# Hybrid decoder layer in split fp32: another order of the seven-product pairs, and eight of them per group instead of seven

## The chip, the cores and the metric

The kernel runs on one core of a Trainium2 chip. The metric is the device time of one execution in microseconds (us). The engines are named as in the profile: PE multiplies matrices, DVE and ACT are the vector and the scalar engine, POOL is GpSimd, SP issues most of the DMA transfers.

## What is computed

One layer over 272 tokens (16 learned ones and 256 given ones) with a model width of 4096, and a last norm:

```
h = rmsnorm(x, norm_g)
q, k, v, g_attn, b_conv, c_conv, h_conv, z_conv = split(h @ w_in)      # 8 x 2048 columns
o = stick_breaking_attention(heads(q), heads(k), heads(v))             # 16 heads x 128
o = group_rmsnorm(o * silu(g_attn), attn_norm_g, ATTN_HEADS)
y = b_conv * short_conv(c_conv * h_conv, conv_w)                       # 16 groups x 128
y = group_rmsnorm(y * silu(z_conv), conv_norm_g, CONV_GROUPS)
x = x + concatenate([o, y]) @ w_out                                    # 4096 x 4096
return rmsnorm(x, final_norm_g)[:, N_META:]
```

All of it is fp32. `w_in` is 4096 x 16384 and `w_out` 4096 x 4096.

## The kernel before

**Split products.** PE multiplies operands of a shorter type (fp32r), so each fp32 operand is split in a high part (a cast, on ACT, L308) and a low part (operand minus high part, on DVE, L309). One product is three matmuls: token low part by weight high part (L340), high by high (L342), high by low (L343).

**Pieces.** The weights come as pieces of 128 x 1024 (512 KB) in one list, `pieces`. For each piece the program loads it (SP, `load`, 8 pieces ahead), splits it (`split`, 5 pieces ahead; `wh` and `wl` have six buffers each, the raw pieces five) and multiplies with it (`mm_in`). A piece is named by a letter, its group and its pair; in the profile it is a number, as in `wl92`. The scheduler of the framework fixes each engine's order of instructions from this program before the run.

**Groups.** Two attention heads and two conv channel groups make one of 8 groups. A group has two stages. In the first, the 32 blocks of 128 model rows are taken as 16 pairs j, each with pieces A and B; the outputs are four PSUM banks (two halves of the tokens by two halves of the columns), `D11`, `D12`, `D21`, `D22`. In the second, eight plain blocks (k, v, c, h of two heads or channel groups) take four pieces of 24 matmuls each (`mm`, L332 to L334).

**Seven products.** A pair of blocks is a 2 x 2 product of blocks: eight products, 24 matmuls of 128 x 512, or seven products, 21 matmuls, with sums of tokens and sums of weights in place of the eighth. The pairs of `SJ` (groups 1 to 7) and of `OUT_SJ` (the output blocks) are done so. They need the token sums `sum{j}` (POOL L228 to L231, then split by ACT L232 and DVE L233), and of the weights, per group: t (L317, 128 x 1024), two more sums of 128 x 512 (L320 and L321), and the splits of T (which is t) and U (the last sum) as pieces of their own. Of B only one half is split. The order of such a pair is A, B, T, U; its products go partly into four more banks, `P1`, `P5`, `P6`, `P7`.

**End of a first stage.** After U of the last seven-product pair, `evict_sums` adds these four banks up (ACT L516, DVE L517 to L520); two more pieces later `evict` (L526) adds them to the four others. The four transposes of `mix` (`mxc`, L570) and the first plain block need banks that L518 and L520 set free.

**Group 0** has no seven-product pairs. There the tokens themselves are prepared: for each j, `prep_x` multiplies a piece of x by the norm's weight (L211, L213) and splits it (L218, L219); if j is in `SJ`, the token sums follow at once. After the pairs 4 to 12 a piece of x in rows is squared for the norm (L281). The sums are kept for all groups.

**Tasks.** All else (gates, scores, weights of the attention, conv, norms, the transposes of the results) is tied to piece numbers by `later`. The results of groups 0 to 6 go to memory (`mixd`) and are loaded again as pieces m; those of group 7 stay. Its `conv_out` (L544, L547) is on POOL, its norm on ACT (L557, L564) and DVE (L559, L173 to L182, L561), and its transposes `mxc7` (L570) stand at piece n1 + 8.

**Output stage.** Three blocks of 1024 output columns, as groups 8, 9 and 10, take 16 pairs each, in the order `OUT_ORDER`; the tokens' place is taken by the results, `mixh` and `mixl`. In group 8 the pieces m4, m5 and m6 come in between; each of them is split (L286, L287), and token sums `osum{j}` are made of it. Loads of the residual and the last norm's weight are issued at two pairs of each block (`load_res`). Then come the last 1024 columns with plain products (`mo`).

Of the kernel before, what the change touches and what calls it, by code (L numbers as in the profile page):

```python
# [17 lines left out]
KC = D // P  # L18
# [7 lines left out]
GROUPS = 8  # L26
# [11 lines left out]
WARM = 10  # L38
LOADS, SPLITS, RING = 8, 5, 6

SJ = (2, 4, 6, 8, 10, 12, 14)


OUT_ORDER = (0, 1, 2, 3, 8, 4, 9, 5, 10, 6, 11, 7, 12, 13, 14, 15)
OUT_SJ = (8, 9, 10, 11, 12, 13)


def seven(g, j):
    return j in (OUT_SJ if g >= GROUPS else SJ if g else ())

# [6 lines left out]
def kernel(ctx, tc, xt, xin, xm, par, fg, w1, w2, out):  # L57
# [35 lines left out]
    pieces = []  # L93
    ends = {}
    fin = {}
    ms = [("m", g) for g in range(GROUPS - 1)]
    for g in range(GROUPS):
        for j in range(KC // 2):
            pieces += [(q, g, j) for q in ("ABTU" if seven(g, j) else "AB")]
            if g == 0 and 4 <= j < 13:  # L100
                pieces.append(("x", j - 4))
        fin[g] = len(pieces) - 1
        for u, b in ((0, 0), (0, 1), (1, 0), (1, 1), (0, 2), (0, 3), (1, 2), (1, 3)):
            for kc in range(4):
                pieces.append(("p", (2 * g + u, b), kc))
            ends.setdefault(g, []).append(len(pieces) - 1)
            if g == GROUPS - 1 and b == 2 + u:
                pieces += ms[2 * u:2 * u + 2]
    n1 = len(pieces)

    for g in range(GROUPS, GROUPS + 3):
        for at_, j in enumerate(OUT_ORDER):
            for q in "ABTU" if seven(g, j) else "AB":
                pieces.append((q, g, j))
                if g == GROUPS and (at_, q) in ((2, "A"), (3, "A"), (9, "A")):
                    pieces.append(ms[{2: 4, 3: 5, 9: 6}[at_]])
        fin[g] = len(pieces) - 1
    for nb in range(6, 9):
        for kc in range(16 if nb < 7 else 8):
# [74 lines left out]
    sp = sctx.enter_context(tc.tile_pool(name="sp", bufs=1))  # L194
    S = {j: sp.tile([P, 2, 4, P], F32R, name=f"sum{j}") for j in SJ}
    xr = {}
# [8 lines left out]
    def prep_x(j, parts=1):  # L205
# [11 lines left out]
        if parts == 1:  # L217
            nc.scalar.copy(out=x[:, :, 0, :], in_=t)  # L218
            nc.vector.tensor_tensor(out=x[:, :, 1, :], in0=t, in1=x[:, :, 0, :].bitcast(F32), op=ALU.subtract)  # L219
        if j in SJ:  # L220
            token_sums(S[j], t[:, :, META:], j)

    def token_sums(dst, t, j):
        a11, a21 = t[:, 0, :P], t[:, 0, P:]
        a12, a22 = t[:, 1, :P], t[:, 1, P:]
        f = wk.tile([P, 4, P], F32, tag="u2", name=f"sf{j}", bufs=2)
        v = nc.gpsimd
        v.tensor_tensor(out=f[:, 0, :], in0=a21, in1=a22, op=ALU.subtract)  # L228
        v.tensor_tensor(out=f[:, 2, :], in0=a11, in1=a21, op=ALU.subtract)
        v.tensor_tensor(out=f[:, 1, :], in0=f[:, 0, :], in1=a11, op=ALU.subtract)  # L230
        v.tensor_tensor(out=f[:, 3, :], in0=a12, in1=f[:, 1, :], op=ALU.add)  # L231
        nc.scalar.copy(out=dst[:, 0], in_=f)  # L232
        nc.vector.tensor_tensor(out=dst[:, 1], in0=f, in1=dst[:, 0].bitcast(F32), op=ALU.subtract)  # L233
# [13 lines left out]
    def load(i):  # L247
        p = pieces[i]
        if p[0] in "TU":
            return  # L250
        if p[:2] == ("A", 0) and p[2] > 0:
            load_x(p[2])
        t = wp.tile([P, 1024], F32, tag="raw", name=f"raw{i}", bufs=5)
        raws[i] = t
        if p[0] == "x":
            if p[1] < 8:
                r, c = divmod(p[1], 4)
                nc.sync.dma_start(out=t, in_=xin[r * P:(r + 1) * P, c * 1024:(c + 1) * 1024])
            else:
                nc.sync.dma_start(out=t[:, :512], in_=xm)  # L260
        elif p[0] == "m":
            nc.sync.dma_start(out=t.rearrange("p (a b) -> p a b", a=4), in_=mixd[p[1]])
        elif i < 2:
            for h in range(2):
                nc.sync.dma_start(out=t[:, 512 * h:512 * h + 512], in_=where[i][:, 512 * h:512 * h + 512])
                if i == 0 and h == 0:
                    nc.sync.dma_start(out=xr[0][:, 1:, :], in_=xt[:, 1:2, :])
        else:
            nc.sync.dma_start(out=t, in_=where[i])
# [131 lines left out]
    def run_tasks(i):  # L401
        ready = [t for t in tasks if t[0] <= i]
        for t in ready:
            tasks.remove(t)
        for t in sorted(ready, key=lambda t: t[0]):
            t[1](*t[2])

    V, A, G, T = nc.vector, nc.scalar, nc.gpsimd, nc.tensor
# [85 lines left out]
    def plain_block(u, b, e):  # L494
        ps = psum.pop((u, b, "p"))
        if b == 0:
            k_block(u, ps[:, :L])
        elif b == 1:
            v_block(u, ps[:, :L], e + 4 if u % 2 == 0 else e + 2)
        elif b == 2:  # L500
            c_block(u, ps[:, META - 2:L])
        else:
            h_block(u, ps[:, META - 2:L], e + 1)


    gr = {}
# [201 lines left out]
    def cols(nb):  # L708
        return (nb * 512, 512) if nb < 7 else (3584 + (nb - 7) * 256, 256)

    def load_res(nb):
        c, w = cols(nb)
        for t in range(2):
            nc.sync.dma_start(out=res[t][:, c:c + w], in_=xin[t * P:(t + 1) * P, c:c + w])
        if nb % 2 == 0 or nb == 7:
            fgs["tile"] = wk.tile([P, 1024], F32, tag="cb1", name=f"fg{nb}")
        o = 512 * (nb % 2) if nb < 7 else 256 * (nb - 7)
        f = fgs["tile"][:, o:o + w]
        nc.sync.dma_start(out=f, in_=fg[:, c:c + w].broadcast_to([P, w]))
        fgs[nb] = f  # L720
# [86 lines left out]
    for i in range(1 - SPLITS, n):  # L807

        ahead = min(4, max(0, i - (n - 16) + 5))
        while loaded < min(i + LOADS + ahead + 1, n):  # L810
            load(loaded)
            loaded += 1
        while halved < min(i + SPLITS + ahead + 1, n):
            split(halved)
            halved += 1
        if i < 0:
            continue
        p = pieces[i]
        if i < n1:
            mm_in(i)  # L820
            if p[0] == "p" and p[2] == 3:
                plain_block(*p[1], i)
            if p[0] == ("U" if p[1] else "B") and p[2] == SJ[-1]:
                evict_sums(p[1])
                if p[1] == GROUPS - 1:
                    open_mix(0)
            if i in fin.values():
                evict(pieces[i][1])
            if i == n1 - 1:
                open_tail()  # L830
        elif p[0] in "ABTU":
            mm_in(i)
            g = p[1]
            if p[0] == "B" and p[2] in (10, 6):
                load_res(2 * (g - GROUPS) + (p[2] == 6))
            if p[0] == "U" and p[2] == OUT_SJ[-1]:
                out_sums(g)
            if i == fin[g]:
                for q, nb, t in ((D11, 0, 0), (D12, 1, 0), (D21, 0, 1), (D22, 1, 1)):
                    psum["o", 2 * (g - GROUPS) + nb, t] = psum.pop((g, q))  # L840
                for nb in range(2):
                    for t in range(2):
                        out_block(2 * (g - GROUPS) + nb, t)
        elif p[0] == "o":
            if "all" not in hd:
                hd["all"], turn[0] = True, 4
            _, nb, kc = p
            final = nb == 8
            mm_out(i, (0,) if final else (0, 1))
            if kc == 3:  # L850
                load_res(nb)
            if kc == (15 if nb < 7 else 7):
                for t in (0,) if final else (0, 1):
                    out_block(nb, t)
        run_tasks(i)
# [8 lines left out]
def _w1(w_in, np):  # L864

    w = w_in.reshape(KC, P, 8, HEADS, P).transpose(2, 3, 1, 0, 4)
    q, k, v, g, b, c, h, z = w
    kinds = (k, v, c, h)
    out = []
    for gr in range(GROUPS):  # L870
        us = 2 * gr, 2 * gr + 1
        n1 = [t[u] for u in us for t in (q, g)]
        n2 = [t[u] for u in us for t in (b, z)]
        for j in range(KC // 2):
            k1, k2 = 2 * j, 2 * j + 1
            out.append(np.concatenate([t[:, k1] for t in n1] + [t[:, k2] for t in n2], axis=1))
            out.append(np.concatenate([t[:, k2] for t in n1] + [t[:, k1] for t in n2], axis=1))
        for u, kind in ((0, 0), (0, 1), (1, 0), (1, 1), (0, 2), (0, 3), (1, 2), (1, 3)):
            for kc in range(4):
                out.append(kinds[kind][us[u]][:, 8 * kc:8 * kc + 8].reshape(P, 1024))  # L880
    return np.ascontiguousarray(np.stack(out))
# [49 lines left out]
```

## Time and profile before

| | |
|---|---|
| runs | 1829.32, 1831.61, 1831.73 us; median 1831.61 us |
| profiled execution | 1833.59 us, of which its span is 1831.7 us |
| mean granted clock of PE | 0.996 |
| PE, DVE, ACT, POOL busy | 1809.7, 1355.4, 1072.8, 111.6 us |
| first stage of group 0 | from 7.49 to 97.84 us |
| first stages of groups 1 to 7, from the first matmul of 128 x 512 to the first of the plain blocks | 83.20, 85.27, 83.16, 83.00, 82.96, 82.96, 83.31 us |
| output blocks 8, 9 and 10 | from 1473.44 to 1731.18 us |

The profile was taken in one execution, and its times count from the start of the span. In a timeline a row has the start, the duration, engine, line, operation, and what is written and read; an "x3" joins three of a kind. Neighbouring instructions of an engine overlap by some 0.08 us, and matmuls by more, so that the step from one start to the next is what an instruction costs. In brackets stands the idle time of the engine before the row and what ended it. A view of windows has for each stretch its length, the busy time of each engine with its number of instructions, the granted clock of PE (1.00 is full), the busy share of the DMA engines and GB/s.

### The profile page before, as it was taken

What the parts mean: (1) busy time and instruction counts of PE and PEld (TensorE: products, weight loads), DVE (VectorE), ACT (ScalarE), POOL (GpSimd) and SP (SyncE); (2) the same over time, 40 slices, a digit from 0 to 9 for tenths busy, and PEclk for the clock granted to TensorE, in tenths of its full rate; (3) what the DMA queues carried; (4) which work ended last, traced back from release to release, by engine and by line L of the source; (5) the groups of instructions that cost most, each with busy time, mean ns of one, the idle gap of its engine ahead of it and who ended that gap; (6) DMA issues with size and microseconds to landing.
All of it is one profiled execution on the core that took longest, in us unless ns stands there. A gap on an engine that the chain in (4) does not pass through costs nothing.

```text
span 1831.7 us, 29345 instructions
## 1 busy us (share of the span) xinstructions
PE 1809.7 (99%) x11121; PEld 1633.6 (89%) x11121; DVE 1355.4 (74%) x1969; ACT 1072.8 (59%) x1653; POOL 111.6 (6%) x172
## 2 busy tenths in 40 slices
PE   9999999999999999999999999999999999999997
PEld 7799889988998899889988998899889977888887
DVE  6686786678667876786678667866786768898953
ACT  6766556655665666556655665566556655555542
POOL 2210001000100010001000100010001031000000
PEclk9999999999999999999999999999999999999999
DMA  8865566446554664466546644755475675665663
GB/s 295 303 213 167 164 219 204 169 161 205 201 173 157 218 207 168 167 220 202 170 159 222 206 169 162 227 195 170 165 231 185 208 261 197 232 227 193 225 216 120
DMA packets 106846, 364.26 MB, mean 199 GB/s; under 512 B 11984, under 2 KB 16848, under 8 KB 106704
## 3 DMA queue, kind: packets, MB, share of 16 engines
q1 hardware_dynamic: 102672, 358.72, 58.7%
q10 hardware_dynamic: 4032, 3.67, 0.6%
q8 instruction: 87, 1.43, 0.3%
q14 instruction: 55, 0.45, 0.1%
HBM read 354.48 MB, written 7.86 MB: 198 GB/s over the span
## 4 chain that ended last, share of the span: by engine, by line
PE 93%; DVE 2%; ACT 1%; DMA 1%; issue 1%; POOL 1%; SPq 0%; POOLq 0%; DVEq 0%; ACTq 0%
PE P L343 15%; PE P L340 15%; PE P L342 15%; PE mm L332 14%; PE mm L333 13%; PE mm L334 13%; PE mo L755 2%; PE mo L756 2%; PE mo L754 2%; DVE wl L309 2%; ACT wh L308 1%; DMA xr<-xt 0%; PE z L602 0%; PE po L648 0%; DMA raw<-xin 0%
## 5 line engine op out<-in xcount | busy, mean ns | idle before, releaser
L309 DVE TENSOR_TENSOR wl<-raw,wh 128x1024 fp32r<-128x1024 f32 (+1 forms) x707 | 810.8, 1172 | 270.9 <-ACT wh L308 257.8
L308 ACT CAST wh<-raw 128x1024 fp32r<-128x1024 f32 (+1 forms) x707 | 690.2, 1005 | 543.0 <-PE mm L333 209.7
L332 PE MATMUL mm<-xs,wh 128*128 128x258 f32 (+1 forms) x2048 | 590.7, 288 | 1.6 <-DVE cb L520 1.5
L333 PE MATMUL mm<-xs,wh 128*128 128x258 f32 (+1 forms) x2048 | 583.3, 285 | 0.0
L334 PE MATMUL mm<-xs,wl 128*128 128x258 f32 (+1 forms) x2048 | 583.1, 285 | 0.0
L332 PEld LDWEIGHTS mm<-xs,wh 128*128 128x128 f32 x2048 | 386.7, 189 | 5.0 <-ACT wh L308 1.6
L333 PEld LDWEIGHTS mm<-xs,wh 128*128 128x128 f32 x2048 | 386.8, 189 | 0.6
L334 PEld LDWEIGHTS mm<-xs,wl 128*128 128x128 f32 x2048 | 386.8, 189 | 0.0
L340 PE MATMUL P<-wh,xs 128*128 128x512 f32 x779 | 304.4, 391 | 2.4 <-ACT wh L308 2.4
L343 PE MATMUL P<-wl,xs 128*128 128x512 f32 x779 | 303.6, 390 | 1.1 <-DVE wl L309 1.1
L342 PE MATMUL P<-wh,xs 128*128 128x512 f32 x779 | 303.4, 390 | 0.0
L340 PEld LDWEIGHTS P<-wh,xs 128*128 128x128 f32 x779 | 146.3, 188 | 32.6 <-ACT wh L308 3.3
L343 PEld LDWEIGHTS P<-wl,xs 128*128 128x128 f32 x779 | 146.3, 188 | 32.4 <-DVE wl L309 1.9
L342 PEld LDWEIGHTS P<-wh,xs 128*128 128x128 f32 x779 | 146.4, 188 | 30.0
L343 PE MATMUL P<-wl,mixh 128*128 128x512 f32 x294 | 115.5, 393 | 0.5 <-DVE wl L309 0.5
L340 PE MATMUL P<-wh,mixl 128*128 128x512 f32 x294 | 115.5, 393 | 0.4 <-ACT wh L308 0.4
L342 PE MATMUL P<-wh,mixh 128*128 128x512 f32 x294 | 115.2, 392 | 0.0
L317 DVE TENSOR_TENSOR t<-raw,raw 128x1024 f32<-128x1024 f32 x67 | 81.9, 1223 | 20.8 <-DMA raw<-w 17.8
L308 ACT CAST wh<-t 128x1024 fp32r<-128x1024 f32 x67 | 70.6, 1054 | 43.6 <-PE P L342 30.4
L309 DVE TENSOR_TENSOR wl<-t,wh 128x1024 fp32r<-128x1024 f32 x67 | 82.1, 1225 | 3.4 <-ACT wh L308 2.6
L340 PE MATMUL P<-wh,sum 128*128 128x512 f32 x196 | 76.3, 390 | 0.0
L342 PE MATMUL P<-wh,sum 128*128 128x512 f32 x196 | 76.3, 389 | 0.0
(243 smaller groups left out, 1806.3 us busy)
## 6 DMA issues: line engine op xcount, KB each, us to landing
raw<-w SPq DMA_DIRECT2D x638, 512.0 KB, 4.0
raw<-xin SPq DMA_DIRECT2D x8, 512.0 KB, 5.0
xr<-xt SPq DMA_DIRECT2D x15, 272.0 KB, 5.2
raw<-mixd SPq DMA_DIRECT2D x7, 512.0 KB, 3.9
res<-xin SPq DMA_DIRECT2D x14, 256.0 KB, 6.1
out<-res SPq DMA_DIRECT2D x4, 512.0 KB, 3.3
mixd<-mfh ACTq DMA_DIRECT2D x14, 128.0 KB, 2.4
mixd<-mfc ACTq DMA_DIRECT2D x14, 128.0 KB, 3.8
```

The lines of the kernel that those rows point to most:

```text
L308: nc.scalar.copy(out=h[:, c], in_=t[:, c])
L309: nc.vector.tensor_tensor(out=lo[:, c], in0=t[:, c], in1=h[:, c].bitcast(F32), op=ALU.subtract)
L317: nc.vector.tensor_tensor(out=s.rearrange("p (a b) -> p a b", a=2), in0=a.rearrange("p (a b) -> p a b", a=2), in1=t[:, 512:].unsqueeze(1). ...
L332: nc.tensor.matmul(out=o, lhsT=h, rhs=x[:, 0, s:], start=k == 0, stop=False)
L333: nc.tensor.matmul(out=o, lhsT=h, rhs=x[:, 1, s:], start=False, stop=False)
L334: nc.tensor.matmul(out=o, lhsT=lo, rhs=x[:, 0, s:], start=False, stop=k == KC - 1)
L340: nc.tensor.matmul(out=o, lhsT=a[1], rhs=h, start=key not in begun, stop=False)
L342: nc.tensor.matmul(out=o, lhsT=a[0], rhs=h, start=False, stop=False)
L343: nc.tensor.matmul(out=o, lhsT=a[0], rhs=lo, start=False, stop=last)
L754: T.matmul(out=o, lhsT=ml, rhs=h, start=m == 0, stop=False)
L755: T.matmul(out=o, lhsT=mh, rhs=h, start=False, stop=False)
L756: T.matmul(out=o, lhsT=mh, rhs=lo, start=False, stop=m == UNITS - 1)
```

## The change

`SJ` has eight pairs in place of seven, 7 to 14. In groups 1 to 7 the pairs are taken in the order `IN_ORDER`, so that the seven-product pairs stand at the places 2, 4, 6, 7, 9, 11, 12 and 14 of 16 (before: 2, 4, 6, 8, 10, 12 and 14); at 6 and 7, and at 11 and 12, two follow each other. Group 0 keeps the order of j, so its token sums are made at j = 7 to 14 in place of 2, 4, 6, ... 14. `OUT_ORDER` has an order for each output block. In block 8 the pair 8 comes a place later and pairs 10 and 11 follow each other; the piece m5 stands after A of the sixth pair in place of the fourth. In blocks 9 and 10 the seven-product pairs stand at the places 2, 4, 6, 8, 10 and 12 in place of 4, 6, 8, 10, 12 and 13. The second `load_res` is issued at pair 11 in place of 6. The host packs the weights in the new orders. One more set of token sums is kept (4 KB per partition).

```diff
-SJ = (2, 4, 6, 8, 10, 12, 14)
-
-
-OUT_ORDER = (0, 1, 2, 3, 8, 4, 9, 5, 10, 6, 11, 7, 12, 13, 14, 15)
+SJ = (7, 8, 9, 10, 11, 12, 13, 14)
+
+IN_ORDER = (0, 1, 7, 2, 8, 3, 9, 10, 4, 11, 5, 12, 13, 6, 14, 15)
+
+
+OUT_ORDER = [(0, 1, 2, 3, 4, 8, 5, 9, 6, 10, 11, 7, 12, 13, 14, 15)] + \
+    2 * [(0, 1, 8, 2, 9, 3, 10, 4, 11, 5, 12, 6, 13, 7, 14, 15)]
 OUT_SJ = (8, 9, 10, 11, 12, 13)
...
-        for j in range(KC // 2):
+        for j in IN_ORDER if g else range(KC // 2):
             pieces += [(q, g, j) for q in ("ABTU" if seven(g, j) else "AB")]
...
-        for at_, j in enumerate(OUT_ORDER):
+        for at_, j in enumerate(OUT_ORDER[g - GROUPS]):
             for q in "ABTU" if seven(g, j) else "AB":
                 pieces.append((q, g, j))
-                if g == GROUPS and (at_, q) in ((2, "A"), (3, "A"), (9, "A")):
-                    pieces.append(ms[{2: 4, 3: 5, 9: 6}[at_]])
+                if g == GROUPS and (at_, q) in ((2, "A"), (5, "A"), (9, "A")):
+                    pieces.append(ms[{2: 4, 5: 5, 9: 6}[at_]])
...
-            if p[0] == "B" and p[2] in (10, 6):
-                load_res(2 * (g - GROUPS) + (p[2] == 6))
+            if p[0] == "B" and p[2] in (10, 11):
+                load_res(2 * (g - GROUPS) + (p[2] == 11))
```

**DVE in the first stage of group 1.** Before, a plain pair stands between two seven-product pairs. The rows are the end of pair 6 (pieces 89 to 92), the plain pair 7 (93, 94), and pair 8 (95 to 98) up to its T:

```order
L321 TENSOR_TENSOR raw89_2344<-raw90_2362,raw89_2344 128x512
L309 TENSOR_TENSOR wl92_2428<-raw89_2344,wh92_2427 128x1024
L309 TENSOR_TENSOR wl93_2446<-raw93_2397,wh93_2445 128x1024
L317 TENSOR_TENSOR t96_2484<-raw95_2425,raw96_2443 128x1024
L309 TENSOR_TENSOR wl94_2462<-raw94_2413,wh94_2461 128x1024
L309 TENSOR_TENSOR wl95_2472<-raw95_2425,wh95_2471 128x1024
L309 TENSOR_TENSOR wl96_2481<-raw96_2443,wh96_2480 128x512
L320 TENSOR_TENSOR raw95_2425<-raw95_2425,t96_2484 128x512
L309 TENSOR_TENSOR wl97_2497<-t96_2484,wh97_2496 128x1024
L321 TENSOR_TENSOR raw95_2425<-raw96_2443,raw95_2425 128x512
```

Now, at the same place of the stage (the lines of the code are three further down), the end of pair 9 (pieces 89 to 92) and pair 10 (93 to 96), two that follow each other:

```order
L324 TENSOR_TENSOR raw89_2352<-raw90_2370,raw89_2352 128x512
L320 TENSOR_TENSOR t94_2471<-raw93_2405,raw94_2421 128x1024
L312 TENSOR_TENSOR wl92_2434<-raw89_2352,wh92_2433 128x1024
L312 TENSOR_TENSOR wl93_2450<-raw93_2405,wh93_2449 128x1024
L323 TENSOR_TENSOR raw93_2405<-raw93_2405,t94_2471 128x512
L312 TENSOR_TENSOR wl94_2468<-raw94_2421,wh94_2467 128x512
L324 TENSOR_TENSOR raw93_2405<-raw94_2421,raw93_2405 128x512
L312 TENSOR_TENSOR wl95_2484<-t94_2471,wh95_2483 128x1024
L312 TENSOR_TENSOR wl96_2493<-raw93_2405,wh96_2492 128x1024
```

The next pair's t now stands between the last sum of pair 9 and the split of its U (wl92), and in pair 10 the last sum stands ahead of the split of T (wl95) in place of behind it. Where a plain pair follows, the order is as before.

**DVE at the norm of group 7's conv half, in block 8.** `ssc7` and `nc7` are the norm's small tiles, `osum10` and `osum11` the token sums of m5, 633 to 636 the pieces of the first seven-product pair. Before:

```order
L233 TENSOR_TENSOR osum10_15612<-sfo10_15613,osum10_15612 128x512
L173 TENSOR_SCALAR nc7_0_15591<-ssc7_15584 128x4
L233 TENSOR_TENSOR osum11_15620<-sfo11_15621,osum11_15620 128x512
L174 TENSOR_SCALAR nc7_1_15592<-nc7_0_15591 128x4
L309 TENSOR_TENSOR wl633_15657<-raw633_15566,wh633_15656 128x1024
L176 TENSOR_TENSOR nc7_2_15593<-nc7_1_15592 128x4
L309 TENSOR_TENSOR wl634_15663<-raw634_15608,wh634_15662 128x512
L177 TENSOR_TENSOR nc7_2_15593<-nc7_2_15593,nc7_0_15591 128x4
L317 TENSOR_TENSOR t634_15666<-raw633_15566,raw634_15608 128x1024
L178 SCALAR_TENSOR_TENSOR nc7_1_15592<-nc7_2_15593,nc7_1_15592 128x4
```

Now (646 is A of the fifth pair, a plain one):

```order
L176 TENSOR_SCALAR nc7_0_15662<-ssc7_15655 128x4
L177 TENSOR_SCALAR nc7_1_15663<-nc7_0_15662 128x4
L589 SCALAR_TENSOR_TENSOR mixl7_15546<-mxh7_15628,pt_84,mixh7_15542 128x256
L179 TENSOR_TENSOR nc7_2_15664<-nc7_1_15663 128x4
L180 TENSOR_TENSOR nc7_2_15664<-nc7_2_15664,nc7_0_15662 128x4
L181 SCALAR_TENSOR_TENSOR nc7_1_15663<-nc7_2_15664,nc7_1_15663 128x4
L182 SCALAR_TENSOR_TENSOR nc7_2_15664<-nc7_1_15663 128x4
L312 TENSOR_TENSOR wl646_15700<-raw646_15610,wh646_15699 128x1024
```

The sums of m5 and the work of the first seven-product pair now stand behind the norm. On PE the 12 matmuls of B of the fourth pair stand ahead of the transposes of `mxc7` now, and behind them before.

**ACT in group 0.** The rows are one pair each, pair 7, from the preparation of x to the square of the next piece of x; before:

```order
L213 ACTIVATE xr7_400<-xr7_400,pt_84 128x272
L218 CAST xs3_127<-xr7_400 128x2x272
L308 CAST wh17_460<-raw17_402 128x1024
L308 CAST wh18_478<-raw18_431 128x1024
L281 ACTIVATE raw19_437,sq9_120<-raw19_437 128x1024
```

Now pair 8, which is like every pair from 7 to 12:

```order
L216 ACTIVATE xr8_432<-xr8_432,pt_84 128x272
L221 CAST xs4_128<-xr8_432 128x2x272
L235 CAST sum8_137<-sf8_492 128x512
L311 CAST wh20_499<-raw20_434 128x1024
L311 CAST wh21_517<-raw21_463 128x1024
L284 ACTIVATE raw22_469,sq9_120<-raw22_469 128x1024
```

The cast of the token sums, which waits for POOL, stood in every second pair and stands in eight pairs in a row now.

More of the change, by code (lines that the diff above doesn't have):

```diff
@@ L873, in _w1 @@
         n2 = [t[u] for u in us for t in (b, z)]
-        for j in range(KC // 2):
+        for j in IN_ORDER if gr else range(KC // 2):
             k1, k2 = 2 * j, 2 * j + 1
@@ L900 @@
     for c in range(0, 3072, 1024):
-        for j in OUT_ORDER:
+        for j in OUT_ORDER[c // 1024]:
             m1, m2 = w[2 * j], w[2 * j + 1]
```

## The prediction

> **What bounds the kernel now.** First the page: the busy line and the chain that ended last.
>
> ```profile
> PE 1809.7 (99%) x11121; PEld 1633.6 (89%) x11121; DVE 1355.4 (74%) x1969; ACT 1072.8 (59%) x1653; POOL 111.6 (6%) x172
> PE 93%; DVE 2%; ACT 1%; DMA 1%; issue 1%; POOL 1%; SPq 0%; POOLq 0%; DVEq 0%; ACTq 0%
> ```
>
> PE is busy 99% of the span, so matmuls that go are time won, as far as nothing else is late. Where that is so is seen by stage, in the view of windows: a piece of group 0, the first stage of group 1, and two short stretches, at the end of group 2's first stage and in output block 8.
>
> ```profile
> 70.00:80.00 10.00, 8.83 (x38) 6.69 (x37) 6.22 (x9) 7.45 (x13) 2.24 (x4) 1.00 0.84 301
> 196.30:279.50 83.20, 83.20 (x371) 68.70 (x369) 70.55 (x87) 47.75 (x62) 2.49 (x4) 1.00 0.60 196
> 463.50:466.90 3.40, 3.36 (x15) 3.40 (x16) 3.40 (x5) 0.00 (x0) 0.00 (x0) 0.51 0.84 299
> 1497.60:1501.10 3.50, 3.50 (x10) 2.73 (x9) 1.41 (x2) 0.78 (x2) 0.00 (x0) 0.51 1.03 348
> ```
>
> A first stage has PE full and DVE at 70.55 of 83.20 us. DVE's 74% over the span hides that here it has little to spare. Twice PE went at half clock (0.51).
>
> DVE's timeline shows its cycle, from the split of one U (first of the x2) to the next, one seven-product and one plain pair later.
>
> ```profile
> 227.70 2.36 DVE L309 TENSOR_TENSOR wl<-raw,wh 128x1024 fp32r<-128x1024 f32 x2 [1.19 <-ACT wh L308]
> 229.97 1.22 DVE L317 TENSOR_TENSOR t<-raw,raw 128x1024 f32<-128x1024 f32 x1
> 231.11 2.96 DVE L309 TENSOR_TENSOR wl<-raw,wh 128x1024 fp32r<-128x1024 f32 x3
> 233.98 0.69 DVE L320 TENSOR_TENSOR raw<-raw,t 128x512 f32<-128x512 f32 x1
> 234.58 1.22 DVE L309 TENSOR_TENSOR wl<-t,wh 128x1024 fp32r<-128x1024 f32 x1
> 235.72 0.69 DVE L321 TENSOR_TENSOR raw<-raw,raw 128x512 f32<-128x512 f32 x1
> 237.60 1.23 DVE L309 TENSOR_TENSOR wl<-raw,wh 128x1024 fp32r<-128x1024 f32 x1 [1.19 <-ACT wh L308]
> ```
>
> From start to start, t costs 1.14 us (229.97 to 231.11), a sum of 128 x 512 0.60, a full split 1.14. A cycle takes 9.90, of which 1.19 is a wait: U's cast on ACT can begin only when L321 is done. How far DVE is ahead of PE is read where PE first uses U's low part: the start of that matmul less the end of the split (its start and 1.22).
>
> ```profile
> 217.78 2.36 DVE L309 TENSOR_TENSOR wl<-raw,wh 128x1024 fp32r<-128x1024 f32 x2 [1.17 <-ACT wh L308]
> 221.78 0.39 PE L343 MATMUL P<-wl,xs 128*128 128x512 f32 x1
> ...
> 267.39 2.36 DVE L309 TENSOR_TENSOR wl<-raw,wh 128x1024 fp32r<-128x1024 f32 x2 [1.19 <-ACT wh L308]
> 272.78 0.39 PE L343 MATMUL P<-wl,xs 128*128 128x512 f32 x1
> ```
>
> The lead is 221.78 - 219.00 = 2.78 us at the second U of the stage and 272.78 - 268.61 = 4.17 at the last. What it is for shows at the end of the stage, in group 1 and then in group 2:
>
> ```profile
> 278.71 0.68 DVE L520 TENSOR_TENSOR cb<-P,cq 128x512 f32<-128x512 f32 x1
> 278.90 0.39 PE L343 MATMUL P<-wl,xs 128*128 128x512 f32 x1
> 279.54 0.36 PE L332 MATMUL mm<-xs,wh 128*128 128x272 f32 x1
> ...
> 461.74 0.41 PE L570 MATMUL mxc<-ident,cb 128*128 128x128 f32 x2 [0.55 <-DVE cq L518]
> 462.71 0.68 DVE L520 TENSOR_TENSOR cb<-P,cq 128x512 f32<-128x512 f32 x1
> 463.54 0.56 PE L332 MATMUL mm<-xs,wh 128*128 128x272 f32 x1 [1.39 <-DVE cb L520]
> ```
>
> In group 1, L520 ends at 279.39, 10.78 us after the split of the last U, and the first plain matmul starts at 279.54, just as PE is through with what stood before it. So a lead of 4.17 is barely enough. In group 2 PE waited 0.55 + 1.39 us for L518 and L520, and then had half clock. From 272.78 to 278.90 there are 27 matmuls: 0.2267 us each.
>
> **The change part by part.** (1) Seven groups lose three matmuls each: 21 x 0.2267 = **4.76 us** less on PE.
>
> (2) A stage gets one more seven-product pair. It costs DVE 1.14 (t) + 2 x 0.60 + 2 x 1.14 (T and U) - 0.54 (half of B) = 4.1 us more, with its wait 5.3. For PE a seven-product pair is 21 x 0.2267 = 4.76, a plain one 5.44, a cycle 10.20: DVE gains 0.30 a cycle now. In the new order the next pair's t (1.14) fills the wait of 1.19 where two pairs follow each other, and in the second of them T's split covers U's cast. That one takes DVE 1.14 (A) + 0.60 (B) + 2 x 0.60 + 2 x 1.14 = 5.22, with 0.07 for what is left of each of two waits 5.36 from U to U, and PE 4.76. Up to the second U (places 2 and 4) nothing changes, so the lead is 2.78 there. From then to the last U come four cycles of 9.90 and two such pairs: DVE 39.6 + 10.72 = 50.32, PE 4 x 10.20 + 2 x 4.76 = 50.32. The lead **stays at 2.78** in place of rising to 4.17; it dips to about 2.5 at the followers, so nothing waits within the stage. After the last U the order is as before, so L520 again ends 10.78 us later and PE waits 4.17 - 2.78 = **1.39 us** at the end of every first stage. Bounds for this unseen wait: 0, if DVE wins the 1.39 back; 0.55 + 1.39 = 1.94 with 1.7 of half clock, as in group 2. I take 1.39, the nearest by its lead. Per group -0.68 + 1.39 = +0.71, in seven groups **+5.0 us** (from -4.8 to +8 or so).
>
> (3) Group 0: where it waits, and ACT's cycle.
>
> ```profile
> 19.69 0.50 PE L343 MATMUL P<-wl,xs 128*128 128x512 f32 x1 [0.53 <-DVE wl L309]
> 74.55 0.50 PE L340 MATMUL P<-wh,xs 128*128 128x512 f32 x1 [0.65 <-ACT wh L308]
> 75.81 0.50 PE L343 MATMUL P<-wl,xs 128*128 128x512 f32 x1 [0.53 <-DVE wl L309]
> ...
> 45.76 0.51 ACT L213 ACTIVATE xr<-xr,pt 128x272 f32<-128x272 f32 x1
> 52.19 0.51 ACT L213 ACTIVATE xr<-xr,pt 128x272 f32<-128x272 f32 x1
> 57.02 0.52 ACT L213 ACTIVATE xr<-xr,pt 128x272 f32<-128x272 f32 x1 [0.17 <-DMA xr<-xt]
> ```
>
> A pair with sums takes ACT 6.43 us (45.76 to 52.19), one without 4.83, PE 5.44. The first wait is behind the sums of pair 2, which go: about -1.0 with its slower restart. Six pairs with sums in a row lose 6 x 0.99 = 5.9 us of lead; the pairs 3 to 6 can build up 4 x 0.6 and what the buffers allow, so the wait near pair 12 (some 1.7) returns, and pairs 13 and 14, now both with sums, add about 1. Bounds: -2.6 (all waits gone) and +2. I take **-0.5**.
>
> (4) Output block 8 waits most:
>
> ```profile
> 1496.34 0.30 PE L570 MATMUL mxc<-ident,cb 128*128 128x128 f32 x1 [2.76 <-ACT cb L564]
> 1496.93 0.53 PE L570 MATMUL mxc<-ident,cb 128*128 128x128 f32 x3 [0.28 <-ACT cb L564]
> ...
> 1522.73 0.62 ACT L232 CAST osum<-sfo 128x512 fp32r<-128x512 f32 x1 [4.25 <-POOL sfo L231]
> 1526.07 0.50 PE L340 MATMUL P<-wh,mixl 128*128 128x512 f32 x1 [0.41 <-ACT wh L308]
> 1527.33 0.50 PE L343 MATMUL P<-wl,mixh 128*128 128x512 f32 x1 [0.53 <-DVE wl L309]
> ```
>
> The transposes of group 7's conv half wait 2.76 + 0.28 us for a norm between whose steps DVE does sums and splits; half clock follows (3.5 us at 0.51, some 1.7 lost). Now 12 matmuls, 2.72 us, stand ahead of them, so that even a norm that is no earlier makes them wait only 0.3; and it comes earlier, with m5 behind it. That is -2.8 to -5, and I take -5: with the wait the half clock goes. The waits at 1526 and 1527, with 0.41 + 0.53 and the slow matmuls around them some 1.5, come after ACT stood for m6's sums (4.25); two smaller ones follow. With two seven-product pairs right behind m6 these 2.3 us become 0 to 4; I take 2. Together **-5.5** (from -7.5 to -1). Blocks 9 and 10 have no waits, and their moved pairs and loads stand beside a full PE: 0; if that cover failed, a wait as in block 8, 1 to 2 us.
>
> The sum is +5.0 - 0.5 - 5.5 = **-1.0 us** on the profiled execution, 1833.59, which lies 1.98 above the median of the runs: 1830.6, so **1830.5**.
>
> The half clock is the point where a rule bears. In group 2 it came after 0.55 + 1.39 us of waiting; after 0.65 + 0.53 in group 0 it did not (1.00 from 70 to 80). The Trainium skill, "TensorE: Matmul & The Clock Gate", section "HAM oscillation — how this bites in real kernels", has the clock fall after idle gaps of more than some 3.4 us. By it, no wait of 1.39 costs clock and the sum stands; the trace doesn't agree, as 1.94 were enough in group 2.
>
> **The rivals.** (A) The matmuls pay in full: DVE reaches its old lead, as its idle time in a stage (12.65 us of 83.20) suggests, and (2) is -4.8. Against it speaks that its waits are tied to ACT and recur in each cycle. Time: 1830.6 - 9.8 = 1821. (B) Slower: the wait at a stage's end passes the point where the clock falls, between 1.2 (group 0) and 1.94 us (group 2). Then each stage costs another 1.7: 7 x 1.7 = 11.9, 1842.5. For it: the lead in group 2 was 1.72 after one late load, and from 2.78 such a load gets there sooner. Against it: with 1.39 we are below 1.94, with matmuls and transposes between. (C) Block 8 gives back what it gained: m6's sums hold ACT (4.25) while two seven-product pairs follow, with waits of 4 us and a half clock: (4) is only -1.5, 1834.5. (D) The eight sums in a row are dearer: group 0 loses 2 instead of winning 0.5, 1833. That the change doesn't do what it says can't be: PE's order has 21 matmuls less.
>
> **How the numbers follow.** Forecast 0.48, A 0.12, B 0.12, C 0.16, D 0.12. The forecast's own range is 1826 to 1835. What a measurement can tell from no change is 0.2%, 3.7 us: 1827.9 and 1835.3. Faster: A and a quarter of the forecast, 0.26; slower: B, a quarter of C, a little of D and of the forecast, 0.2; within: 0.54. The range for 8 in 10 leaves out the far end of A and most of B: 1823 to 1839.
>
> **What would show it.** In the new profile: at the end of each of the seven first stages, PE idle before L335 (332 before) for some 1.4 us, released by L523 (520), at full clock; a lead of 2.8 at the last U; no wait before mxc7; no wait at 19.7 in group 0, but waits between 70 and 90; no half clock at 1497. A lead near 4 would show A right, digits of half clock at stage ends B, waits of PE behind m6 C. The prediction is wrong if the lead at the last U isn't near 2.8, or if DMA, whose landings I took as unchanged, comes late at the new places.

## The result, and the profile after

The changed kernel takes 1841.20 us (median of four runs, 1837.94 to 1844.09), the kernel before 1831.01 us (four runs): ratio 1.0057, 95% interval 1.0045 to 1.0069. On a second chip it was 1.0050 (1.0038 to 1.0062). It is 10 us slower, clear of the 0.2%, and outside the stated range.

The profiled execution took 1839.95 us (span 1838.2), 6.4 us more than the profiled one of before. From the first and the last matmul of each stage the two compare so:

| stage | before | after | difference | forecast |
|---|---|---|---|---|
| group 0, end of its first stage | 97.84 | 100.01 | +2.2 | -0.5 |
| first stages of groups 1 to 7, summed | 583.86 | 589.33 | +5.5 | +5.0 |
| plain stages, summed | 791.75 | 790.47 | -1.3 | 0 |
| output blocks 8 to 10 | 257.73 | 257.86 | +0.1 | -5.5 |
| last 1024 columns | 89.75 | 89.75 | 0.0 | 0 |

They add up to 6.5. The rest of the 10 us lies in which execution was profiled: that of before stands 2.6 above its median (the 1.3 us that its plain stages take more come from a half clock in group 2), that of after 1.3 below.

The waits of PE in groups 1 to 7 (engine, line, what was waited for; then the sum, the times and the longest in us):

```profile
PE mm L335 <- DVE cb L523: 9.3, 7, 1.4
PE mxc L573 <- DVE cq L521: 2.0, 2, 1.7
PE po L647 <- ACT at L450: 0.4, 1, 0.4
```

Before, the first of these lines was 1.5 us in the whole run:

```profile
PE mm L332 <- DVE cb L520: 1.5, 2, 1.4
```

Now each of the seven stages ends with it, and inside the stages PE waits for nothing. The end of group 1's stage in the timeline, with the split of the last U (first of the x6) and its first use:

```profile
270.61 6.90 DVE L312 TENSOR_TENSOR wl<-raw,wh 128x1024 fp32r<-128x1024 f32 x6 [1.19 <-ACT wh L311]
274.25 0.39 PE L346 MATMUL P<-wl,xs 128*128 128x512 f32 x1
280.60 0.38 PE L573 MATMUL mxc<-ident,cb 128*128 128x128 f32 x2
281.52 0.68 DVE L523 TENSOR_TENSOR cb<-P,cq 128x512 f32<-128x512 f32 x1
282.35 0.36 PE L335 MATMUL mm<-xs,wh 128*128 128x272 f32 x1 [1.37 <-DVE cb L523]
```

The lead at the last U is 274.25 - (270.61 + 1.22) = 2.42 us, where it was 4.17. L523 ends 10.4 us after that split, and PE waits 1.37.

In group 0, ACT's timeline:

```profile
50.50 0.51 ACT L216 ACTIVATE xr<-xr,pt 128x272 f32<-128x272 f32 x1
51.35 0.65 ACT L221 CAST xs<-xr 128x544 fp32r<-128x544 f32 x1 [0.35 <-DVE xr L214]
53.76 0.62 ACT L235 CAST sum<-sf 128x512 fp32r<-128x512 f32 x1 [1.75 <-POOL sf L234]
...
57.23 0.51 ACT L216 ACTIVATE xr<-xr,pt 128x272 f32<-128x272 f32 x1
```

A pair with sums behind another such pair takes ACT 6.73 us (50.50 to 57.23), not 6.43: DVE, which has to split the sums too, is 0.35 late with the next x. In this execution PE then waits for ACT or DVE at pairs 10 to 13. The wait at 19.7 is gone, as forecast.

In block 8 the timeline of SP, PE and DVE (SP's duration is that of issuing):

```profile
1499.37 2.82 SPq L717 DMA_DIRECT2D res<-xin  x4
1503.82 0.33 SPq L272 DMA_DIRECT2D raw<-w  x1
1504.19 1.38 SPq L717 DMA_DIRECT2D res<-xin  x3
...
1502.51 0.60 PE L573 MATMUL mxc<-ident,cb 128*128 128x128 f32 x4
...
1509.59 1.23 DVE L320 TENSOR_TENSOR t<-raw,raw 128x1024 f32<-128x1024 f32 x1 [4.70 <-DMA res<-xin]
1510.73 0.48 DVE L589 SCALAR_TENSOR_TENSOR mixl<-mxc,pt,mixh 128x256 fp32r<-128x256 f32 x1
...
1512.88 0.47 PE L343 MATMUL P<-wh,osum 128*128 128x512 f32 x1 [2.28 <-DVE mixl L589]
1534.52 0.50 PE L343 MATMUL P<-wh,osum 128*128 128x512 f32 x1 [0.97 <-ACT wh L311]
1541.26 0.50 PE L343 MATMUL P<-wh,osum 128*128 128x512 f32 x1 [0.71 <-ACT wh L311]
```

The transposes of mxc7 no longer wait, and no half clock follows. But DVE stands 4.70 us before t of pair 9, whose piece raw656 was issued at 1503.82 among the loads of the residual; behind it in DVE's queue is the low part of mxc7 (L589), and PE waits 2.28 for that. At pairs 10 and 11, right behind m6, there are waits again, now at two pairs.

The same two rows of DVE before the change:

```profile
1499.69 1.23 DVE L317 TENSOR_TENSOR t<-raw,raw 128x1024 f32<-128x1024 f32 x1 [2.79 <-DMA res<-xin]
1501.97 0.48 DVE L586 SCALAR_TENSOR_TENSOR mixl<-mxc,pt,mixh 128x256 fp32r<-128x256 f32 x1
```

So the late load of pair 9 and the low part behind it were there before too (DVE stood 2.79 us), but PE, which had waited 2.8 us for the norm shortly before, did not wait for them.

### The profile page after: what moved, and what is told of

It reads as the page before. It is cut to its first block, busy times and chain, and to the rows that moved or that the text cites. A ratio compares the mean times of both kernels' runs of the same rounds, so it can differ in the third digit from the quotient of the medians.

```text
span 1838.2 us, 29390 instructions
## 1 busy us (share of the span) xinstructions
PE 1804.7 (98%) x11100; PEld 1626.2 (88%) x11100; DVE 1388.3 (76%) x2005; ACT 1081.4 (59%) x1668; POOL 109.3 (6%) x176
## 4 chain that ended last, share of the span: by engine, by line
PE 89%; DVE 4%; DMA 2%; issue 1%; ACT 1%; POOL 1%; SPq 0%; DVEq 0%; POOLq 0%; ACTq 0%
PE P L346 14%; PE P L345 14%; PE P L343 14%; PE mm L335 14%; PE mm L336 13%; PE mm L337 13%; DVE wl L312 3%; PE mo L758 2%; PE mo L757 2%; PE mo L759 2%; DMA raw<-w 1%; ACT wh L311 1%; PE z L605 0%; DVE t L320 0%; PE po L651 0%
## 5 line engine op out<-in xcount | busy, mean ns | idle before, releaser
L346 PE MATMUL P<-wl,xs 128*128 128x512 f32 x744 | 290.0, 390 | 2.5 <-DVE wl L312 2.5
L343 PE MATMUL P<-wh,xs 128*128 128x512 f32 x744 | 290.9, 391 | 1.5 <-ACT wh L311 1.5
L345 PE MATMUL P<-wh,xs 128*128 128x512 f32 x744 | 289.5, 389 | 0.0
L346 PEld LDWEIGHTS P<-wl,xs 128*128 128x128 f32 x744 | 139.7, 188 | 33.6 <-DVE wl L312 4.7
L343 PEld LDWEIGHTS P<-wh,xs 128*128 128x128 f32 x744 | 139.7, 188 | 31.6 <-ACT wh L311 3.3
L345 PEld LDWEIGHTS P<-wh,xs 128*128 128x128 f32 x744 | 139.7, 188 | 28.5
L311 ACT CAST wh<-t 128x1024 fp32r<-128x1024 f32 x74 | 78.0, 1053 | 63.2 <-DVE t L320 31.1
L320 DVE TENSOR_TENSOR t<-raw,raw 128x1024 f32<-128x1024 f32 x74 | 90.3, 1220 | 19.2 <-DMA raw<-w 14.5
L312 DVE TENSOR_TENSOR wl<-t,wh 128x1024 fp32r<-128x1024 f32 x74 | 90.1, 1218 | 0.8
L346 PE MATMUL P<-wl,sum 128*128 128x512 f32 x224 | 87.2, 389 | 0.0
L345 PE MATMUL P<-wh,sum 128*128 128x512 f32 x224 | 87.2, 389 | 0.0
```

Of the source, the lines that this page charges most:

```text
L311: nc.scalar.copy(out=h[:, c], in_=t[:, c])
L312: nc.vector.tensor_tensor(out=lo[:, c], in0=t[:, c], in1=h[:, c].bitcast(F32), op=ALU.subtract)
L320: nc.vector.tensor_tensor(out=s.rearrange("p (a b) -> p a b", a=2), in0=a.rearrange("p (a b) -> p a b", a=2), in1=t[:, 512:].unsqueeze(1). ...
L343: nc.tensor.matmul(out=o, lhsT=a[1], rhs=h, start=key not in begun, stop=False)
L345: nc.tensor.matmul(out=o, lhsT=a[0], rhs=h, start=False, stop=False)
L346: nc.tensor.matmul(out=o, lhsT=a[0], rhs=lo, start=False, stop=last)
```

## The experiments

All ran in five rounds against the kernel before on the same chip; the ratios are to that.

**The last seven-product pair one place earlier.**

```diff
-IN_ORDER = (0, 1, 7, 2, 8, 3, 9, 10, 4, 11, 5, 12, 13, 6, 14, 15)
+IN_ORDER = (0, 1, 7, 2, 8, 3, 9, 10, 4, 11, 5, 12, 13, 14, 6, 15)
```

> The changed kernel with the last two places of the first stages swapped: the eighth seven-product pair stands at place 13, a plain pair at 14 (..., 12, 13, 14, 6, 15). Same number of matmuls, same DVE work. Theory (the wait at each stage's end is the fixed 10.8 us of DVE work after the last U, less the lead): PE has 5.44 us more to do after the last U, so all seven waits before L335 (9.3 us in all, released by L523) and those before the transposes (2.0) go, about -10 to -11 us against the changed kernel, some 1830 to 1832. Rival (DVE has too much work in a stage, and the wait only moves): PE waits for wl inside the stage in place of its end, the time stays within 2 us of the changed kernel.

Measured: 1826.09 us, 0.9982 of before (0.9973 to 0.9991). All waits of PE in groups 1 to 7:

```profile
PE po L647 <- ACT at L450: 0.4, 1, 0.4
```

The seven stages take 82.13 to 82.48 us (before 82.96 to 85.27), although DVE does the same work in them as in the changed kernel. Against the ratios of the changed kernel that is 12 to 14 us, somewhat more than expected. Between the two profiles the first stages differ by 13.6 us (11.3 of it are the waits, those of group 3 among them, where a late load had cut the lead to 0.63 at the last U), group 0 by 1.4; plain stages and output blocks take 1.1 and 1.0 more. So the slowdown in these stages was the place of the last pair, not DVE's load.

**The other way: the last one at place 15.**

```diff
-IN_ORDER = (0, 1, 7, 2, 8, 3, 9, 10, 4, 11, 5, 12, 13, 6, 14, 15)
+IN_ORDER = (0, 1, 7, 2, 8, 3, 9, 10, 4, 11, 5, 12, 13, 6, 15, 14)
```

> The changed kernel with the last two places of the first stages swapped the other way: the plain pair 15 at place 14, the seven-product pair 14 at 15. Theory (10.8 us of DVE work after the split of the last U, against the lead and what PE has left after U): two plain pairs in a row raise the lead from 2.4 to about 5.5 us at the last U, but PE has only 1.2 us left after it in place of 6.65, so it waits 10.8 - 5.5 - 1.2 = 4.1 us a stage in place of 1.65: seven times 2.5 more, +17 us against the changed kernel, more if the clock falls. Rival (the waits come from DVE's load as a whole, which is the same): within 3 us of the changed kernel.

Measured: 1833.49 us, 1.0018 (1.0010 to 1.0027): 5.7 us below the changed kernel on the same chip, where the theory had 17 more and the rival no more than 3 either way. PE and DVE at the end of group 1's stage:

```profile
271.00 1.22 DVE L312 TENSOR_TENSOR wl<-raw,wh 128x1024 fp32r<-128x1024 f32 x1
278.26 0.39 PE L346 MATMUL P<-wl,xs 128*128 128x512 f32 x1
...
278.94 0.39 PE L346 MATMUL P<-wl,sum 128*128 128x512 f32 x1
279.16 0.29 PE L335 MATMUL mm<-xs,wh 128*128 128x272 f32 x1
279.29 0.28 PE L336 MATMUL mm<-xs,wh 128*128 128x272 f32 x1
280.48 0.39 PE L337 MATMUL mm<-xs,wl 128*128 128x272 f32 x1 [0.91 <-DVE wl L312]
...
283.88 0.68 DVE L523 TENSOR_TENSOR cb<-P,cq 128x512 f32<-128x512 f32 x1
```

The lead at the last U was 278.26 - (271.00 + 1.22) = 6.0 us (5.5 expected), and L523 ended 5.4 us after PE's last product. But PE's order was another one: the scheduler put a piece of a plain block (24 matmuls of 128 x 272) that doesn't wait for L523 ahead of the transposes, so that PE waited only 0.91 for its split. The amount failed since the expectation took PE's order as fixed. What PE would wait with the order of the changed kernel wasn't tried, so this run says nothing against the theory and little for it.

**The sums alone.** The kernel before, with other pairs at the same places (SJ = 8 to 14), so that only group 0 changes.

```diff
-SJ = (2, 4, 6, 8, 10, 12, 14)
+SJ = (8, 9, 10, 11, 12, 13, 14)
+IN_ORDER = (0, 1, 8, 2, 9, 3, 10, 4, 11, 5, 12, 6, 13, 7, 14, 15)
...
-        for j in range(KC // 2):
+        for j in IN_ORDER if g else range(KC // 2):
...
```

> The kernel before with only the names of the pairs changed: seven seven-product pairs 8 to 14 stand at the places 2, 4, ... 14 as before, so nothing changes in groups 1 to 7 and in the output, and group 0 makes its sums at 8 to 14 in a row. Theory: group 0's first stage is 2 to 2.7 us longer (about 92.7 us) with waits between 65 and 84 us, and the time is up by as much against before. Rival (DMA bound): within 0.7 us of before.

Measured: 1828.13 us, 0.9997 (0.9988 to 1.0005). Group 0's first stage ended at 97.87 us (before 97.84). The theory (2 to 2.7 us longer) falls: that seven sums come late and in a row costs nothing by itself. The first wait goes, the chain of ACT is as long, and ends at the same time.

**Every second pair again, with an eighth at pair 15.**

```diff
-SJ = (7, 8, 9, 10, 11, 12, 13, 14)
-IN_ORDER = (0, 1, 7, 2, 8, 3, 9, 10, 4, 11, 5, 12, 13, 6, 14, 15)
+SJ = (2, 4, 6, 8, 10, 12, 14, 15)
+IN_ORDER = (0, 1, 2, 3, 4, 5, 6, 8, 7, 10, 9, 12, 14, 11, 15, 13)
```

> The changed kernel with the same places of the seven-product pairs, but other pairs standing there: 2, 4, 6, 8, 10, 12, 14 and 15, so that group 0 makes its token sums at every second pair as before, and at 15. Theory (in group 0 ACT takes 6.7 us for each pair with sums, and six such pairs with a square in a row pace PE): the five waits of PE between 62 and 84 us shrink to those of before, group 0's first stage goes from 93.1 to about 90.5 us, -2.5 us against the changed kernel. Rival (group 0 is bound by its DMA, the order of the sums only moves the waits): within 0.7 us of the changed kernel. Stage ends as in the changed kernel in both.

Measured: 1839.68 us, 1.0059 (1.0046 to 1.0072), no less than the changed kernel (1.0057 and 1.0050). The 2.5 us of the theory are not seen. Its group 0 ended at 98.67 us, within what the kernels with eight sums in a row show (97.96 to 100.01 in eight profiles, 99.05 in the mean). Where in that range a run ends is set early: in the changed kernel's profile ACT waited 1.10 us for a piece of x at 36.28, in last_at_13 it didn't, was 1.4 us earlier at pair 7, and ended 1.4 us earlier. In all eight the stage ends 62.7 us (62.66 to 62.70) after ACT begins pair 7, which is at 35.3 to 37.3 us: from there on ACT's chain alone sets the end.

**Sums where no square is.** From last_at_13 on:

```diff
-SJ = (7, 8, 9, 10, 11, 12, 13, 14)
-IN_ORDER = (0, 1, 7, 2, 8, 3, 9, 10, 4, 11, 5, 12, 13, 14, 6, 15)
+SJ = (3, 5, 7, 9, 11, 13, 14, 15)
+IN_ORDER = (0, 1, 3, 2, 5, 4, 7, 9, 6, 11, 8, 13, 14, 15, 10, 12)
```

> last_at_13 with other pairs at the same places: 3, 5, 7, 9, 11, 13, 14, 15, so that group 0 makes its sums at every second pair up to 11 and then at the three pairs that have no square of x. Theory (group 0 ends when ACT's chain of casts, squares and sums ends): five chains of sums before pair 12 in place of six, group 0's first stage ends at about 97.3 us in place of 98.6 to 100.0, time 1 to 2.5 us below last_at_13. Rival (DMA sets the end of group 0): within 0.7 us.

Measured: 1823.80 us, 0.9971 (0.9960 to 0.9982). Group 0's stage ended at 95.75 us, 2.9 before last_at_13's 98.64. Its waits of PE in group 0:

```profile
PE P L346 <- DVE wl L312: 0.5, 1, 0.5
PE P L343 <- ACT wh L311: 0.2, 1, 0.2
```

That ACT's chain ends group 0 fits the fixed 62.7 us above; DMA moves the same bytes. The ends go with how many pairs have both sums and a square of x: four here (ends of 95.75 to 96.75 us in three profiles), five before, in late_sums_alone and in sums_spaced (97.84 to 98.67), six in the changed kernel (97.96 to 100.01). The ranges of five and six overlap, and no run changes this number alone, so the count is a reading that fits and not shown by itself. By the ratios the time is 2.0 us below last_at_13, as expected, though the two intervals overlap.

**The output's order of before**, with the place of m5 and the issue of load_res of before, in the changed kernel:

```diff
-OUT_ORDER = [(0, 1, 2, 3, 4, 8, 5, 9, 6, 10, 11, 7, 12, 13, 14, 15)] + \
-    2 * [(0, 1, 8, 2, 9, 3, 10, 4, 11, 5, 12, 6, 13, 7, 14, 15)]
+OUT_ORDER = (0, 1, 2, 3, 8, 4, 9, 5, 10, 6, 11, 7, 12, 13, 14, 15)
...
```

> The changed kernel with the order of the output blocks, the place of m5 and the issue of load_res of before. Theory (block 8 won 5 us at the transposes of mxc7 and lost as much at 1510 and 1533 to 1542): within 1 us of the changed kernel, with the wait before mxc7 back and those at 1510 gone. Rival (the output order is a good part of the slowdown): 3 us or more faster than the changed kernel.

Measured: 1837.60 us, 1.0055 (1.0042 to 1.0067), the changed kernel's ratio; output blocks 256.83 us against 257.86. The waits before mxc7 are back (2.8 and 0.3 us), with half clock. So the output's change wins one wait and makes others of the same size.

**The residual's loads held back.** From last_at_13 on:

```diff
         for t in range(2):
+            if nb > 1:
+                nc.gpsimd.tensor_copy(out=res[t][:, c:c + 1], in_=acc[t])
             nc.sync.dma_start(out=res[t][:, c:c + w], in_=xin[t * P:(t + 1) * P, c:c + w])
```

> last_at_13 with one thing more: the residual's loads of the columns from 1024 on are held until the first output block is done (a copy of one column on POOL from a number made there). In last_at_13 all 14 of them (256 KB each) go out in one stretch around the load of raw656. Theory (block 8 lost its gain because the load of raw656 comes late behind these loads, with DVE's sum t656 waiting for it and the low part of mxc7 behind that): the wait of PE for mixl L589 (3.1 us in last_at_13, with half clock after it) shrinks by 1.5 us or goes, and the time is 2 to 5 us below last_at_13. Rival (raw656 is late because its buffer comes free late, the residual has no part): the wait stays within 0.7 us, the time within 1 us of last_at_13.

Measured: 1824.81 us, 0.9974 (0.9964 to 0.9984); output blocks 255.95 us, where last_at_13 had 258.88. First last_at_13, SP and DVE around the second seven-product pair:

```profile
1485.89 2.52 SPq L717 DMA_DIRECT2D res<-xin  x4
1490.34 0.33 SPq L272 DMA_DIRECT2D raw<-w  x1
1490.71 1.38 SPq L717 DMA_DIRECT2D res<-xin  x3
...
1496.56 1.23 DVE L320 TENSOR_TENSOR t<-raw,raw 128x1024 f32<-128x1024 f32 x1 [5.14 <-DMA res<-xin]
```

Then residual_late:

```profile
1485.11 6.33 SPq L272 DMA_DIRECT2D raw<-w  x3
1491.53 0.86 SPq L724 DMA_DIRECT2D fg<-fg  x2
...
1494.44 1.23 DVE L320 TENSOR_TENSOR t<-raw,raw 128x1024 f32<-128x1024 f32 x1 [2.28 <-DMA raw<-w]
```

DVE's wait falls from 5.14 to 2.28, PE's wait for L589 from 3.1 to 0.5, and the half clock behind it is gone. Against last_at_13 the time is 0.8 parts in a thousand less (1.5 us), below the 2 to 5 expected, above the rival's 1, and within the two intervals; the traces are the better witness here. last_at_13 is the worst of its kind, though. In the six profiles with this order of block 8 and the loads not held, t starts 4.6 to 6.2 us after the issue of its load, DVE waits 3.6 to 5.1 us and PE 1.0 to 3.1 (2.1 in the mean); in the two with the loads held (this one and three_parts below) it is 3.3, 2.2 to 2.3 and 0.4 to 0.5. So the residual's loads do delay that piece, and holding them is worth some 1.7 us of PE's wait.

**The bank freed by ACT.** From last_at_13 on, in mix_out for group 7:

```diff
-                A.mul(out=h, in_=p, mul=gn)
-                V.scalar_tensor_tensor(out=lo, in0=p, scalar=gn, in1=h.bitcast(F32), op0=ALU.mult, op1=ALU.subtract)
+                m = wk.tile([P, SEQ], F32, tag="u2", name=f"mf{q}{g}_{u}", bufs=2)
+                A.mul(out=m, in_=p, mul=gn)
+                A.copy(out=h, in_=m)
+                V.tensor_tensor(out=lo, in0=m, in1=h.bitcast(F32), op=ALU.subtract)
```

> last_at_13, with the results of group 7 first copied from the bank to a tile by ACT; high and low part are made from that tile, so that DVE, which stands before t656, no longer holds the bank that T of the first seven-product pair needs. Two more ACT operations for each of the two halves. Theory (the wait at that place is DVE's queue order, in front of a bank): the wait for mixl L589 goes, a rest of at most 1 us remains for the split of U, which stands behind t656 too; time 2 to 5 us below last_at_13, the half clock at that place gone. Rival (PE needs the split of U at the same moment anyway): the wait only moves to L346 with the same length, within 1 us of last_at_13.

Measured: 1825.44 us, 0.9977 (0.9968 to 0.9986), not told apart from last_at_13; output blocks 256.54 us. The wait for L589 is gone, but mxc7 waits 1.6 us for its norm again: with the changed code the scheduler put the sums of m5 and pair 8 between the norm's steps on DVE, as before the change. Neither side's account held.

**m6 earlier**, from bank_freed_by_act on:

```diff
-OUT_ORDER = [(0, 1, 2, 3, 4, 8, 5, 9, 6, 10, 11, 7, 12, 13, 14, 15)] + \
+OUT_ORDER = [(0, 1, 2, 3, 4, 8, 5, 9, 6, 7, 10, 11, 12, 13, 14, 15)] + \
...
-                if g == GROUPS and (at_, q) in ((2, "A"), (5, "A"), (9, "A")):
-                    pieces.append(ms[{2: 4, 5: 5, 9: 6}[at_]])
+                if g == GROUPS and (at_, q) in ((2, "A"), (5, "A"), (7, "A")):
+                    pieces.append(ms[{2: 4, 5: 5, 7: 6}[at_]])
```

> bank_freed_by_act with m6 two pairs earlier (after A of pair 9 in place of 10), and the plain pair 7 before pair 10, so that 10, 11, 12 and 13 follow each other. Theory (the waits of 1.5 to 4 us at pairs 10 and 11 come from ACT standing for m6's token sums with seven-product pairs right behind): they go or fall below 1.5 us, 1 to 3 us less than bank_freed_by_act. Rival (four seven-product pairs in a row cost the lead again, 0.7 each): waits before T and U of pairs 12 and 13 of the same sum, within 1 us.

Measured: 1824.52 us, 0.9972 (0.9961 to 0.9982); output blocks 256.64 us, as without it. The waits at pairs 10 and 11 went, others came behind m6's new place (1.3 us) and at the later pairs, to the same sum: within 1 us of bank_freed_by_act, as the rival had it.

**Together.** last_at_13, with the pairs of sums_beside_no_square and the loads of residual_late:

> last_at_13 with the pairs of sums_beside_no_square and the residual's late loads of residual_late. If the parts are independent: 1823.8 less what residual_late won (1.3 to 2.9 us in block 8), about 1822, 0.996 of before. If they aren't, no less than sums_beside_no_square.

Measured: 1822.91 us, 0.9964 (0.9951 to 0.9977), near the 1822 of independent parts. Group 0 ended at 96.69, the output blocks took 255.79 us. And with m6's edit of above, but the banks as they were:

> three_parts with m6 two pairs earlier and pairs 10, 11, 12 and 13 one after the other, as in m6_earlier. Theory: the waits of 4 us at pairs 10 and 11 in block 8 come from m6's token sums and go, 1 to 3 us less than three_parts. Rival (m6_earlier's trace: the waits stay, at other pairs): within 1 us of three_parts.

Measured: 1820.59 us, 0.9950 (0.9938 to 0.9962); output blocks 254.29 us, 1.5 less. This is the fastest version: 0.5% below before. Its waits of PE in the output blocks:

```profile
PE P L343 <- DVE mixl L589: 1.5, 1, 1.5
PE P L346 <- DVE wl L312: 0.7, 1, 0.7
PE P L343 <- ACT wh L311: 0.7, 1, 0.7
```

Here m6's new place did help, by 2.3 us at the median (the two intervals still overlap), though the wait for L589 is back at 1.5. Why it helps here and not on top of bank_freed_by_act is not shown.

**The changed kernel once more**, as a base on the chip of the last runs:

> The changed kernel itself, on the chip of the two runs beside it, as a base for them. From its four runs: 1.0045 to 1.0069 of before.

Measured: 1839.19 us, 1.0050 (1.0038 to 1.0062).

## Why the prediction was wrong, point by point

**Part (1)**, 21 matmuls less, was right: in last_at_13, without the waits, a first stage takes 82.2 us where it took 83.0; three matmuls are 0.68 of that, and 0.14 moved into the plain stage.

**Part (2)** was right in its mechanism and nearly in size: +5.0 forecast, +5.5 measured. The lead at the last U is 2.4 to 2.6 us in six groups, in place of 2.78, and 0.63 in group 3: a pair behind another costs the lead 0.72 (2.97 to 2.24 at the first follower of group 1), not 0.60. The waits at the ends were forecast at 1.39 each and are 11.3 us for seven, 9.3 before the plain block and 2.0 before the transposes, the latter mostly in group 3 after a late load. That the place of the last pair makes them is shown by last_at_13. The closeness of the sizes is in part luck: L523 ended 10.2 to 11.0 us after the split of the last U, 10.5 in the mean, where the sum took 10.78, and that made up for most of the shorter lead. And by group the difference runs from -1.7 (group 2, whose late load of before is gone) to +2.6 us (group 3, where there is one now); the other five show +0.6 to +1.4, where +0.71 was forecast. The upper bound of +8 left out the half clock that its own sentence adds to the 1.94.

**Part (3)** failed by its sizing: -0.5 forecast, with +2 as its bound, +2.2 measured. The sum had the cycle with sums at 6.43; behind another it is 6.73. And it counted the first wait as time won, although ACT's chain, which ends the stage, is no shorter for it: late_sums_alone shows that the order of seven sums is worth nothing by itself, and sums_beside_no_square that other pairs for the eight sums are worth 2 to 3 us. In the mean of eight profiles the end is 1.2 us later than before; the profiled one was the latest of them.

**Part (4)** is the step that failed most: -5.5 forecast, +0.1 measured, 5.6 of the 7.5 us by which the sum missed the profile. With it right, the profile would have been 0.9 us slower in place of 6.5. That the wait and the half clock at mxc7 go was right (no wait there in the profile after). The step that failed is the overlap behind them: the sum counted the wait's whole length as won, and took the landings of DMA as unchanged and harmless, which the prediction itself named as the condition that could break it. The t of pair 9 stands in DVE's queue ahead of the low part of mxc7, its piece comes behind the residual's loads, and PE needs the bank: 2.28 us of waiting. The row with 2.79 us of before shows that this load was late already then, with the same low part behind it, where PE, itself held up by the norm, did not meet it: the profile of before had the second wait in it, one queue further back. residual_late and three_parts show the loads' share: with them later, DVE waits 2.2 to 2.3 us in place of 3.6 to 5.1. Rival C put the price of block 8 on m6 alone, at 1.5 us still won. The second loss, at pairs 10 and 11 behind m6 (0.97, 0.70, 0.71 and 0.70 us), is the one that C named.

**The rivals.** B was nearest in time, 1842.5, but not by its mechanism: in the profile after no half clock followed any stage end (granted clock 1.00), and where one did in other runs it was in the one group with a late load. The other three executions of the changed kernel have mean granted clocks of 0.996 and 0.997 where the profiled one has 0.998, so some half clock in them isn't excluded. A was wrong for the changed kernel, as the lead didn't come back. D had the direction of group 0 right and, in the profiled execution, its size.

**The base.** The forecast was set against a profiled execution and moved to the median of three runs, 1831.61, by 1.98 us; the four runs of the result have 1831.01. The two profiled executions stand 2.6 above and 1.3 below their medians, so that 3.8 of the 10.2 us are not in the comparison of the two traces.

## What to carry to other kernels

Where a run of buffers is freed by a fixed chain of one engine, ask how much work the waited-for engine still has after the chain's start: moving the last item by one place was worth more here than the item itself. A wait that goes is worth its length only if what comes next isn't behind the same queue: list what stands behind it on that engine, with each load that must land first. And code that leaves a scheduler free is not the old order with one thing changed; look at the new order of every engine before a sum is made of old durations.

## What the runs showed of the hardware

The half clock was expected from about 1.9 us of waiting on. In these two rows of the changed kernel, PE waits 1.68 and 1.38 us in group 3, and the clock stays:

```profile
647.41 0.41 PE L573 MATMUL mxc<-ident,cb 128*128 128x128 f32 x2 [1.68 <-DVE cq L521]
649.20 0.36 PE L335 MATMUL mm<-xs,wh 128*128 128x272 f32 x1 [1.38 <-DVE cb L523]
...
649.20:652.60 3.40, 3.40 (x28) 3.40 (x29) 3.40 (x5) 0.28 (x1) 0.00 (x0) 1.00 0.73 251
```

In changed_again, at the same place with 2.50 and 1.38 us, it falls to 0.50 for more than 3.5 us:

```profile
648.23 0.41 PE L573 MATMUL mxc<-ident,cb 128*128 128x128 f32 x2 [2.50 <-DVE cq L521]
650.02 0.57 PE L335 MATMUL mm<-xs,wh 128*128 128x272 f32 x1 [1.38 <-DVE cb L523]
...
649.90:653.40 3.50, 3.38 (x15) 3.41 (x16) 3.50 (x5) 0.00 (x0) 0.00 (x0) 0.50 0.60 224
```

Before the change 0.55 and 1.39 us were enough. In block 8, single waits of 2.28 (the changed kernel) and 2.35 us (last_at_15) passed at 1.00, and waits of 2.62 (changed_again, 0.57 in the 3.4 us behind it) and 3.14 us (last_at_13, 0.50) did not. So the length of the waits alone doesn't decide. The Trainium skill, "TensorE: Matmul & The Clock Gate", section "What's actually happening", has the clock set by activity in windows of 3.4 us that run on their own; that waits of 3.1 us pass once and 1.9 us don't at another time agrees with a window whose phase differs, but no run here shows where the windows lie. None of the waits was as long as the 3.4 us that its section "HAM oscillation — how this bites in real kernels" gives as the gap to avoid.
